# The opening of a two-layer decoder trunk: first input block in two transfers, its weights on another queue, products on half the tokens

## The chip, the cores and the metric

The kernel runs on one core of a Trainium2 chip. The metric is the device time of one execution in microseconds (us). Several executions are timed and their median counts; one more execution is recorded by the hardware profiler, and every row shown here comes from such a record.

## The reference

Two layers of a causal decoder trunk on 512 tokens of width 1024. Only the start matters here: the input is normalized by its root mean square, scaled by a gain per channel, and multiplied with the input weights of layer 0.

```python
def rms_norm(x, g):
    x32 = x.astype(jnp.float32)
    y = x32 * lax.rsqrt(jnp.mean(x32 * x32, axis=-1, keepdims=True) + EPS)
    return y.astype(x.dtype) * g

# layer 0, with x of shape (1, 512, 1024) and w_in_even[0] of shape (1024, 2048)
xn = rms_norm(h, norm_mix[0])
proj = jnp.einsum('bsd,de->bse', xn, w_in_even[0])
z_b = proj[..., 3 * A_WIDTH:]          # columns 1536 to 2047: computed first by the kernel
...
# then: gated convolution and causal pooling, an output projection, a gated ConvFFN;
# layer 1: chunked spatial gating and a second gated ConvFFN; a final rms_norm
```

All of it is float32.

## The kernel before

A product of two float32 matrices is made of three products of 32-bit values rounded for TensorE ("fp32r"): each operand is split into a high part (`hi`, a rounded copy) and a low part (`lo`, the rest), and high x high, high x low and low x high are added up in a PSUM bank. Splitting is work for ScalarE and VectorE.

The first stage computes z, columns 1536 to 2047 of the projection, channel by token: four PSUM banks `z`, one for each 128 columns, each of 512 tokens. The sum runs over eight blocks of 128 input channels. For a block k the kernel

- loads `xt`, the block's 128 channels of all 512 tokens (token-major, four groups of 128 tokens), and `raw_z`, the block's 128 x 512 weights (`load`, L373); blocks 0 and 1 alone, the others in pairs;
- turns the block channel-major by four TensorE transposes (`turn`, L390, transposes at L399);
- splits it, scaled by the gain: high part on ScalarE (L419), low part on VectorE (L432), into `hg`; the unscaled block is copied to `h` (L440);
- splits the weights into `whi_z` and `wlo_z` (L422, L426, L417 for the high part, L414 for the low part);
- issues its twelve products, four banks times three kinds. For blocks 0 and 1 these are written out in `z_first` (L452, products at L459), kind by kind, with the next block's `turn` between the first kind and the second; later blocks go through `group` (L163) and `mm3` (L158).

The normalization's factor is applied to z afterwards, so the sums of squares are gathered beside the products (L209).

The first block differs. Its gain column comes in a small transfer of its own (`first_gain`, L366), since the table of all gains (`pkmix`, L104) has to be transposed on TensorE first (L110). Its turned block lies in two banks of 256 tokens: ScalarE scales the second half while VectorE rounds the weights (L422) and then scales the first half (L424). Its products wait for both halves.

Before any data is there, TensorE multiplies a tile `idle` that VectorE has cleared (L56): eight fillers of 512 columns at the start and three of 256 after the first transposes (`keep_busy`, L58):

```python
WARM = (8, 512)
STAY = (3, 256)
```

The order on each engine is fixed by hand in this stage: whatever passes through `inorder` keeps its place in the program's order on its engine. The transfers of the stage are issued by SP, those of `first_gain` and `pkmix` by ScalarE's queue. Transfers take turns on eight semaphores, so an issue can wait for the transfer eight places earlier.

Of the kernel before, what the change touches and what calls it, by code (L numbers as in the profile page):

```python
# [22 lines left out]
EPS = 1e-6  # L23
WINDOWS = (2, 4, 8, 16)
PAD = 16
WARM = (8, 512)
STAY = (3, 256)
LINE = 64


# [1 line left out]
def tile_trunk(ctx: ExitStack, tc: tile.TileContext, x, norm_mix, norm_ffn, final_norm,  # L32
# [19 lines left out]
    inorder = tc.keep_in_program_order  # L52


    idle = tp.tile([P, 512], BF16, tag="rstd", name="idle")
    nc.vector.memset(idle, 0.0)  # L56

    def keep_busy(bank, n, cols):  # L58

        for i in range(n):  # L60
            inorder(nc.tensor.matmul(bank[:, :cols], idle[:, :P], idle[:, :cols], start=i == 0,
                                     stop=i == n - 1))

    keep_busy(aux_bank("clock"), *WARM)
# [23 lines left out]

    eps = small[:, 1:2]
    nc.gpsimd.memset(eps, EPS)  # L90
    nc.scalar.activation(tp.tile([P, LINE], F32, tag="sd", bufs=1, name="sd_0")[:, :1], eps, AF.Sqrt)
# [4 lines left out]
    def params(layer, rows_, order=lambda ins: ins):  # L96
        return params_fetch(layer, rows_, nc.sync)(order)

    def params_fetch(layer, rows_, queue):
        rows = sum(n for _, _, n in rows_)  # L100
        pk = cp.tile([P, P], F32, tag="pk", bufs=1, name=f"pk{layer}")
        at, views = 0, {}
        for key, ap, n in rows_:
            queue.dma_start(pk[at : at + n, :], ap)  # L104
            views[key] = at
            at += n

        def turned(order=lambda ins: ins):
            ps = aux_bank(f"prm_ps{layer}")
            order(nc.tensor.transpose(ps[:, :rows], pk[:rows, :], ident[:rows, :rows]))  # L110
# [16 lines left out]
        return ap.rearrange("w (r p) -> (w r) p", p=P)  # L127


    def fetch(src, a, b, name):  # L130
        raw = wp.tile([P, a, b], F32, tag="raw", bufs=4, name=f"raw_{name}")
        nc.sync.dma_start(raw, src)
        return raw, a, b, name

    def weights(src, a, b, name):
# [22 lines left out]
    def mm3(ps, lhs, rhs, start, stop):  # L158
        nc.tensor.matmul(ps, lhs[0], rhs[0], start=start, stop=False)  # L159
        nc.tensor.matmul(ps, lhs[0], rhs[1], start=False, stop=False)  # L160
        nc.tensor.matmul(ps, lhs[1], rhs[0], start=False, stop=stop)  # L161

    def group(name, outs, ks, lhs, rhs, tail, on_done, before=None, at_end=None, begun=None):  # L163

        start, banks = begun or (0, {})
        head = max(0, len(ks) - tail)
        order = [(i, j) for i in range(start, head) for j in outs]  # L170
        order += [(i, j) for j in outs for i in range(head, len(ks))]
        at = start - 1
        for i, j in order:
            if i > at and before is not None:
                before(ks[i])
            at = max(at, i)
            if j not in banks:
                banks[j] = mm_bank(f"{name}_{j}")
            mm3(banks[j], lhs(ks[i], j), rhs(ks[i], j), i == 0, i == len(ks) - 1)
# [144 lines left out]

    prm0 = prm1 = None

    def in_fetch(name, w, c0, k, n):
        return fetch(w[k * P : (k + n) * P, c0 : c0 + 512].rearrange("(k p) c -> p k c", p=P),
                     n, 512, f"{name}_{k}")

    def in_parts(chunks, k, raw, after=(None, None)):
        hi, lo = parts(*raw, after=after)
# [28 lines left out]
    def mixer0():  # L361
        nonlocal prm0
        w = w_in_even[0]
        with tc.tile_pool(name="m0", bufs=1) as mp:
            first_gain = tp.tile([P, LINE], F32, tag="ms", bufs=1, name="first_gain")[:, :1]
            nc.scalar.dma_start(first_gain, norm_mix[0][:P].rearrange("(p o) -> p o", o=1))  # L366
            prm_mix = {"turned": params_fetch("mix", [("mix", rows_of(norm_mix[0]), NK)],
                                              nc.scalar)}
            norm = Norm("m0", lambda k: prm_mix["col"]("mix", k))
            zchunks = {}  # L370
            xt = {}

            def load(k, n):  # L373
                t = mp.tile([P, NT, n * P], F32, tag="four", bufs=5, name=f"xt{k}")
                nc.sync.dma_start(
                    t, x[:, k * P : (k + n) * P].rearrange("(t p) d -> p t d", p=P))
# [7 lines left out]
            def put_square(ins):  # L384
                fed[1] = inorder(ins)

            for k, n in ((0, 1), (1, 1), (2, 2), (4, 2)):
                load(k, n)

            def turn(k):  # L390
                order = inorder if k < 3 else lambda ins: ins
                split_at = HALF if k == 0 else S
                banks = [mm_bank(f"xt_ps{k}_{i}") for i in range(S // split_at)]

                def turned_(cs):
                    return banks[cs.start // split_at][:, cs.start % split_at :][:, : cs.stop - cs.start]

                for t in range(NT):
                    order(nc.tensor.transpose(turned_(slice(t * P, (t + 1) * P)), xt[k][:, t, :],  # L399
                                              ident))  # L400
                pieces = [slice(i, i + split_at) for i in range(0, S, split_at)]
                if k == 0:
                    keep_busy(mm_bank("busy"), *STAY)
                if k in raws:
                    raw, a, b, name = raws.pop(k)
                    hi = wp.tile([P, a, b], F32R, tag="whi", bufs=6, name=f"whi_{name}")
                    lo = wp.tile([P, a, b], F32R, tag="wlo", bufs=6, name=f"wlo_{name}")
                    for i in range(a):
                        zchunks[k + i] = hi[:, i, :], lo[:, i, :], raw[:, i, :]
                whi, wlo, wraw = zchunks[k]  # L410
                g = prm_mix["col"]("mix", k) if k else first_gain

                def low_weights():
                    inorder(nc.vector.tensor_tensor(wlo, wraw, whi.bitcast(F32), ALU.subtract))  # L414

                if k > 2:
                    inorder(nc.scalar.activation(whi, wraw, AF.Copy))  # L417
                for cs in pieces[-1:]:
                    inorder(nc.scalar.activation(hg[k][0][:, cs], turned_(cs), AF.Copy, scale=g))  # L419
                if k == 0:  # L420
                    for cs in (slice(0, 256), slice(256, 512)):
                        inorder(nc.vector.tensor_copy(whi[:, cs], wraw[:, cs]))  # L422
                    cs = pieces[0]
                    inorder(nc.vector.tensor_scalar_mul(hg[k][0][:, cs], turned_(cs), g))  # L424
                elif k <= 2:
                    inorder(nc.scalar.activation(whi, wraw, AF.Copy))  # L426
                else:
                    low_weights()
                if k == 0:
                    low_weights()  # L430
                for cs in pieces:
                    fed[0] = inorder(nc.vector.scalar_tensor_tensor(  # L432
                        hg[k][1][:, cs], turned_(cs), g, hg[k][0].bitcast(F32)[:, cs],
                        op0=ALU.mult, op1=ALU.subtract))
                if 0 < k <= 2:
                    low_weights()
                if k == 0:
                    prm_mix["col"] = prm_mix["turned"](inorder)
                for cs in pieces:
                    inorder(nc.vector.tensor_copy(h[k][:, cs], turned_(cs)))  # L440
                if k > 0:
                    norm.square(k - 1, put_square)
                if k == 0:
                    load(6, 2)
                elif k == NK - 1:
                    norm.square(k, put_square)

            def ahead(k):
# [3 lines left out]
            def z_first():  # L452

                banks = {j: mm_bank(f"z_{j}") for j in range(4)}
                turn(0)
                for k in range(2):
                    for n, (l, r) in enumerate(((0, 0), (1, 0), (0, 1))):
                        for j in range(4):
                            inorder(nc.tensor.matmul(  # L459
                                banks[j], zchunks[k][l][:, j * P : (j + 1) * P], hg[k][r],  # L460
                                start=k == n == 0, stop=False))
                        if n == 0:
                            turn(k + 1)
                return banks
# [1138 lines left out]
```

## Time and profile before

| | us |
|---|---|
| median of 3 timed runs | 967.64 |
| the three runs | 967.56, 967.64, 969.01 |
| the profiled execution's own time | 967.45 |
| its span, first to last instruction | 965.7 |
| TensorE busy in the span | 956.8 |
| first real product starts, in the span | 6.07 |

Times inside the profile count from the start of the span. A row of the timeline gives start, length, engine, line and operation, the tile written and the tiles read, the shape and the count, and in brackets the idle time before it with what ended it. PE is TensorE's products, PEld its weight loads, DVE is VectorE, ACT is ScalarE; SPq and ACTq are the queues of SP and ScalarE on which transfers are issued.

### The profile page before, as it was taken

The numbers are of one execution on the slowest core, as the hardware profiler recorded it, in microseconds if no ns is written. First come the engines' busy times: TensorE is split into PE (matmuls) and PEld (weight loads), VectorE is DVE, ScalarE is ACT, GpSimd is POOL, SyncE is SP. The second block draws the span as 40 slices with busy tenths as digits, with TensorE's granted clock in tenths as the row PEclk, the third lists the DMA queues.
The fourth block names the chain that finished last, engine by engine and source line by source line (L and its number), as shares of the span: only waits on it lengthen the run. The fifth ranks groups of instructions, "written<-read, shape, count | busy, mean of one in ns | idle before, by whom it ended". The sixth has DMA issues, their size and how long they took to land.

```text
span 965.7 us, 14233 instructions
## 1 busy us (share of the span) xinstructions
PE 956.8 (99%) x5152; PEld 827.2 (86%) x5152; DVE 847.4 (88%) x1437; ACT 621.6 (64%) x942; POOL 162.5 (17%) x184
## 2 busy tenths in 40 slices
PE   9999999999999999999999999999999999999996
PEld 7888898998888888888888888989888888888885
DVE  6887988989899998998878689889998989889897
ACT  5524667766576565765487847787665666646776
POOL 2142323111011010110311002311111011100123
PEclk9999999999999999999999999999999999999998
DMA  7442345777677577774352323467767777657775
GB/s 253 147 140 87 66 145 118 176 191 191 162 179 177 147 177 193 170 179 133 130 153 88 109 88 88 142 142 176 187 150 190 193 175 174 177 150 196 196 153 142
DMA packets 95538, 150.47 MB, mean 156 GB/s; under 512 B 5252, under 2 KB 61036, under 8 KB 95468
## 3 DMA queue, kind: packets, MB, share of 16 engines
q1 hardware_dynamic: 78140, 98.69, 31.2%
q0 software_dynamic: 15696, 49.03, 28.0%
q10 hardware_dynamic: 1632, 1.84, 0.6%
q8 instruction: 41, 0.67, 0.3%
q14 instruction: 29, 0.24, 0.1%
HBM read 98.42 MB, written 2.10 MB: 104 GB/s over the span
## 4 chain that ended last, share of the span: by engine, by line
PE 99%; DVE 1%; ACT 0%; issue 0%; ACTq 0%
PE dn L159 3%; PE d L159 3%; PE dn L160 3%; PE d L160 3%; PE d L161 3%; PE dn L161 3%; PE vu_a L1145 2%; PE gu L159 2%; PE gu L161 2%; PE gu L160 2%; PE u_2a L696 1%; PE g_2a L696 1%; PE u_4a L696 1%; PE u_20a L686 1%; PE u_16a L686 1%; PE u_18a L686 1%
## 5 line engine op out<-in xcount | busy, mean ns | idle before, releaser
L146 POOL DMA_DIRECT2D wlo_g<-raw_g x20 | 17.2, 860 | 312.3 <-DVE kept L923 142.6
L732 DVE SCALAR_TENSOR_TENSOR c<-rows,prm,c 128x512 f32<-128x512 f32 x88 | 65.5, 747 | 1.7 <-ACT c L730 1.4
L159 PE MATMUL d<-a_hi,whi_d 128*128 128x512 f32 x144 | 56.1, 390 | 0.0
L159 PE MATMUL dn<-whi_dn,a_hi 128*128 128x512 f32 x144 | 56.1, 390 | 0.0
L160 PE MATMUL d<-a_lo,whi_d 128*128 128x512 f32 x144 | 56.1, 390 | 0.0
L160 PE MATMUL dn<-wlo_dn,a_hi 128*128 128x512 f32 x144 | 56.1, 390 | 0.0
L161 PE MATMUL d<-a_hi,wlo_d 128*128 128x512 f32 x144 | 56.1, 389 | 0.0
L161 PE MATMUL dn<-whi_dn,a_lo 128*128 128x512 f32 x144 | 56.1, 389 | 0.0
L847 ACT ACTIVATE whi_a<-raw_g 128x512 fp32r<-128x512 f32 x20 | 12.6, 631 | 61.0 <-PE g_10e L686 8.5
L730 ACT ACTIVATE c<-rows,prm 128x512 f32<-128x512 f32 x44 | 31.4, 716 | 14.9 <-DVE rows L947 14.9
L1350 DVE SCALAR_TENSOR_TENSOR y<-dn,small,y 128x512 f32<-128x512 f32 x40 | 28.0, 749 | 7.9 <-PE dn L161 7.8
L740 ACT ACTIVATE s<-c,prm 128x512 f32<-128x512 f32 x44 | 31.4, 716 | 3.3 <-DVE c L732 3.3
L155 DVE TENSOR_TENSOR wlo_dn<-raw_dn,whi_dn 128x1024 fp32r<-128x1024 f32 x18 | 22.0, 1223 | 11.5 <-ACT whi_dn L154 11.5
L204 ACT ACTIVATE hg<-h,prm 128x512 fp32r<-128x512 f32 x24 | 17.2, 719 | 22.9 <-DVE h L317 17.0
L161 PEld LDWEIGHTS dn<-whi_dn,a_lo 128*128 128x128 f32 x144 | 27.0, 188 | 5.6
L161 PEld LDWEIGHTS d<-a_hi,wlo_d 128*128 128x128 f32 x144 | 27.1, 188 | 5.6
L159 PEld LDWEIGHTS dn<-whi_dn,a_hi 128*128 128x128 f32 x144 | 27.1, 188 | 5.6
L160 PEld LDWEIGHTS d<-a_lo,whi_d 128*128 128x128 f32 x144 | 27.1, 188 | 5.6
L160 PEld LDWEIGHTS dn<-wlo_dn,a_hi 128*128 128x128 f32 x144 | 27.1, 188 | 5.5
L159 PEld LDWEIGHTS d<-a_hi,whi_d 128*128 128x128 f32 x144 | 27.1, 188 | 5.5
L268 ACT ACTIVATE a_hi<-s 128x512 fp32r<-128x512 f32 x40 | 24.7, 625 | 10.7 <-PE d L161 9.4
L144 ACT ACTIVATE wlo_g<-raw_g 128x1024 fp32r<-128x1024 f32 x20 | 20.9, 1048 | 16.3 <-PE g_2e L696 7.7
(1274 smaller groups left out, 3380.9 us busy)
## 6 DMA issues: line engine op xcount, KB each, us to landing
raw_g<-in_w_ffn_gate_dram SPq DMA_DIRECT2D x40, 512.0 KB, 3.6
raw_u<-in_w_ffn_up_dram SPq DMA_DIRECT2D x40, 512.0 KB, 4.3
raw_dn<-in_w_ffn_down_dram SPq DMA_DIRECT2D x22, 512.0 KB, 4.5
wlo_g<-raw_g POOLq DMA_DIRECT2D x20, 512.0 KB, 4.6
wlo_u<-raw_u POOLq DMA_DIRECT2D x20, 512.0 KB, 5.8
raw_d<-in_w_ffn_down_dram SPq DMA_DIRECT2D x18, 512.0 KB, 4.1
wlo_s12g<-s12g POOLq DMA_DIRECT2D x18, 512.0 KB, 5.3
wlo_s34g<-s34g POOLq DMA_DIRECT2D x18, 512.0 KB, 5.0
```

Of the source, the lines that this page charges most:

```text
L144: first = nc.scalar.activation(lo, raw, AF.Copy, scale=-1.0)
L155: behind(nc.vector.tensor_tensor(lo, raw, hi.bitcast(F32), ALU.subtract), after[0])
L159: nc.tensor.matmul(ps, lhs[0], rhs[0], start=start, stop=False)
L160: nc.tensor.matmul(ps, lhs[0], rhs[1], start=False, stop=False)
L161: nc.tensor.matmul(ps, lhs[1], rhs[0], start=False, stop=stop)
L268: nc.scalar.activation(hi, src, AF.Copy, scale=scale)
L686: last_matmul[0] = nc.tensor.matmul(ps if low else banks[at], left(kp)[low], right(kp)[0] if low else both(kp), start=first, stop=kp == NP ...
L696: nc.tensor.matmul(ps, l, r, start=first, stop=end, skip_group_check=True)
L730: nc.scalar.activation(c, t[:, 0:S], AF.Copy, scale=prm("cf", ft))
L732: self.last_conv = nc.vector.scalar_tensor_tensor(c, t[:, i : S + i], prm("cf", i * NF + ft), c, op0=ALU.mult, op1=ALU.add)
L740: self.last_silu = nc.scalar.activation(s, c, AF.Silu, bias=self.prm("bf", ft))
L1350: return nc.vector.scalar_tensor_tensor(dst, ps, ffn.cols[:, t : t + 1], dst, op0=ALU.mult, op1=ALU.add)
```

## The change

The change concerns the first block of the z stage and what comes before it.

- The fillers read a constant (1.0 in bfloat16, broadcast) that is set up with the program, and the tile `idle` with its clearing goes. There are six of 512 columns, not eight, and two of 256, not three.
- Block 0 is loaded in two transfers of 256 tokens each, both from SP. The block's weights are issued on ScalarE's queue, between the gain column and the gain table; on SP their place is taken by the second half.
- `turn_first` takes the place of `turn(0)`. TensorE's order is: two transposes of the first half, two fillers, two transposes of the second half, four products of 128x256 on the first half, four on the second, the transpose of the gain table, then the second block's transposes. Before, it was four transposes, three fillers, the gain table, four products of 128x512, the second block's transposes.
- VectorE scales the first half first and then rounds the right half of the weights; ScalarE rounds the left half of the weights and then scales the second half of the block. Before, VectorE rounded both halves of the weights first, and ScalarE none.
- The small square root that loads ScalarE's table is issued after the three transfers on that queue.

The diff, cut to its core:

```diff
-WARM = (8, 512)
-STAY = (3, 256)
+WARM = (6, 512)
+STAY = (2, 256)
...
-    idle = tp.tile([P, 512], BF16, tag="rstd", name="idle")
-    nc.vector.memset(idle, 0.0)
-
     def keep_busy(bank, n, cols):
 
         for i in range(n):
-            inorder(nc.tensor.matmul(bank[:, :cols], idle[:, :P], idle[:, :cols], start=i == 0,
+            inorder(nc.tensor.matmul(bank[:, :cols], nc.const_aps.tensor(1.0, [P, P], BF16),
+                                     nc.const_aps.tensor(1.0, [P, cols], BF16), start=i == 0,
                                      stop=i == n - 1))
...
             def load(k, n):
                 t = mp.tile([P, NT, n * P], F32, tag="four", bufs=5, name=f"xt{k}")
-                nc.sync.dma_start(
-                    t, x[:, k * P : (k + n) * P].rearrange("(t p) d -> p t d", p=P))
+                rows = x[:, k * P : (k + n) * P].rearrange("(t p) d -> p t d", p=P)
                 for i in range(n):
                     xt[k + i] = t[:, :, i * P : (i + 1) * P]
-                raws[k] = in_fetch("z", w, 1536, k, n)
+                if k == 0:
+                    inorder(nc.sync.dma_start(t[:, :2], rows[:, :2]))
+                    raws[k] = in_fetch("z", w, 1536, k, n, nc.scalar, inorder)
+                    inorder(nc.sync.dma_start(t[:, 2:], rows[:, 2:]))
+                    return
+                inorder(nc.sync.dma_start(t, rows))
+                raws[k] = in_fetch("z", w, 1536, k, n, nc.sync, inorder)
...
+            def turn_first(banks):
+                chunk(0)
+                whi, wlo, wraw = zchunks[0]
+                halves = [slice(0, HALF), slice(HALF, S)]
...
+                def high_products(i):
+                    for j in range(4):
+                        inorder(nc.tensor.matmul(
+                            banks[j][:, halves[i]], whi[:, j * P : (j + 1) * P],
+                            hg[0][0][:, halves[i]], start=i == 0, stop=False,
+                            skip_group_check=True))
+
+                transposed(0)
+                inorder(nc.vector.tensor_scalar_mul(hg[0][0][:, halves[0]], turned_[0], first_gain))
+                keep_busy(mm_bank("busy"), *STAY)
+                inorder(nc.scalar.activation(whi[:, halves[0]], wraw[:, halves[0]], AF.Copy))
+                inorder(nc.vector.tensor_copy(whi[:, halves[1]], wraw[:, halves[1]]))
+                transposed(1)
+                high_products(0)
+                inorder(nc.scalar.activation(hg[0][0][:, halves[1]], turned_[1], AF.Copy,
+                                             scale=first_gain))
+                inorder(nc.vector.tensor_tensor(wlo, wraw, whi.bitcast(F32), ALU.subtract))
+                high_products(1)
+                for i in range(2):
+                    low_part(0, turned_[i], first_gain, halves[i])
+                prm_mix["col"] = prm_mix["turned"](inorder)
+                for i in range(2):
+                    inorder(nc.vector.tensor_copy(h[0][:, halves[i]], turned_[i]))
+                load(6, 2)
...
-                turn(0)
+                turn_first(banks)
                 for k in range(2):
                     for n, (l, r) in enumerate(((0, 0), (1, 0), (0, 1))):
-                        for j in range(4):
-                            inorder(nc.tensor.matmul(
-                                banks[j], zchunks[k][l][:, j * P : (j + 1) * P], hg[k][r],
-                                start=k == n == 0, stop=False))
+                        if n or k:
+                            for j in range(4):
+                                inorder(nc.tensor.matmul(
+                                    banks[j], zchunks[k][l][:, j * P : (j + 1) * P], hg[k][r],
+                                    start=False, stop=False, skip_group_check=True))
```

More of the change, by code (lines that the diff above doesn't have):

```diff
@@ L97, in params, with params_fetch @@
         return params_fetch(layer, rows_, nc.sync)(order)
-    def params_fetch(layer, rows_, queue):
+    def params_fetch(layer, rows_, queue, first=lambda ins: ins):
         rows = sum(n for _, _, n in rows_)
@@ L103, in params_fetch @@
         for key, ap, n in rows_:
-            queue.dma_start(pk[at : at + n, :], ap)
+            first(queue.dma_start(pk[at : at + n, :], ap))
             views[key] = at
@@ L127, in conv_rows, with fetch @@
         return ap.rearrange("w (r p) -> (w r) p", p=P)
-    def fetch(src, a, b, name):
+    def fetch(src, a, b, name, queue=nc.sync, order=lambda ins: ins):
         raw = wp.tile([P, a, b], F32, tag="raw", bufs=4, name=f"raw_{name}")
-        nc.sync.dma_start(raw, src)
+        order(queue.dma_start(raw, src))
         return raw, a, b, name
@@ L385, in put_square, with chunk @@
                 fed[1] = inorder(ins)
-            for k, n in ((0, 1), (1, 1), (2, 2), (4, 2)):
-                load(k, n)
+            load(0, 1)
+            prm_mix["turned"] = params_fetch("mix", [("mix", rows_of(norm_mix[0]), NK)], nc.scalar,
+                                             inorder)
+            inorder(nc.scalar.activation(work("sd", 1, "0"), eps, AF.Sqrt))
+            for k, n in ((1, 1), (2, 2), (4, 2)):
+                load(k, n)
+            def chunk(k):
+                raw, a, b, name = raws.pop(k)
+                hi = wp.tile([P, a, b], F32R, tag="whi", bufs=6, name=f"whi_{name}")
+                lo = wp.tile([P, a, b], F32R, tag="wlo", bufs=6, name=f"wlo_{name}")
+                for i in range(a):
+                    zchunks[k + i] = hi[:, i, :], lo[:, i, :], raw[:, i, :]
@@ new lines, in low_part, with transposed @@
+            def low_part(k, ps, g, cs=slice(0, S)):
+                return inorder(nc.vector.scalar_tensor_tensor(
+                    hg[k][1][:, cs], ps, g, hg[k][0].bitcast(F32)[:, cs],
+                    op0=ALU.mult, op1=ALU.subtract))
+            def turn_first(banks):
+                chunk(0)
+                whi, wlo, wraw = zchunks[0]
+                halves = [slice(0, HALF), slice(HALF, S)]
+                turned_ = []
+                for c in halves:
+                    ps = mm_bank(f"xt_ps0_{c.start}")[:, :HALF]
+                    turned_.append(ps)
+                def transposed(i):
+                    for t in range(2):
+                        inorder(nc.tensor.transpose(turned_[i][:, t * P : (t + 1) * P],
+                                                    xt[0][:, 2 * i + t, :], ident))
+                def high_products(i):
[21 more added lines that the diff above has]
+                load(6, 2)
@@ L390, in turn @@
             def turn(k):
                 order = inorder if k < 3 else lambda ins: ins
[L392 to L396, printed above, removed]
+                ps = mm_bank(f"xt_ps{k}")
                 for t in range(NT):
-                    order(nc.tensor.transpose(turned_(slice(t * P, (t + 1) * P)), xt[k][:, t, :],
-                                              ident))
@@ L401, in turn @@
-                pieces = [slice(i, i + split_at) for i in range(0, S, split_at)]
-                if k == 0:
-                    keep_busy(mm_bank("busy"), *STAY)
-                if k in raws:
[L405 to L409, printed above, removed]
+                    order(nc.tensor.transpose(ps[:, t * P : (t + 1) * P], xt[k][:, t, :], ident))
@@ L410, in turn @@
+                if k in raws:
+                    chunk(k)
                 whi, wlo, wraw = zchunks[k]
-                g = prm_mix["col"]("mix", k) if k else first_gain
+                g = prm_mix["col"]("mix", k)
                 def low_weights():
@@ L417, in turn @@
                     inorder(nc.scalar.activation(whi, wraw, AF.Copy))
[L418 to L425, printed above, removed]
+                inorder(nc.scalar.activation(hg[k][0], ps, AF.Copy, scale=g))
+                if k <= 2:
                     inorder(nc.scalar.activation(whi, wraw, AF.Copy))
@@ L428, in turn @@
                     low_weights()
-                if k == 0:
+                fed[0] = low_part(k, ps, g)
+                if k <= 2:
                     low_weights()
[L431 to L445, printed above, removed]
+                inorder(nc.vector.tensor_copy(h[k], ps))
+                norm.square(k - 1, put_square)
+                if k == NK - 1:
                     norm.square(k, put_square)
```

18 lines of the change are left out of this document (8 added, 10 removed).

## The prediction

> **What bounds the kernel now.** I read the page first, then the chain of work that ended last, TensorE's waits, and the timeline of the first 13 us.
>
> ```profile
> span 965.7 us, 14233 instructions
> ...
> PE 956.8 (99%) x5152; PEld 827.2 (86%) x5152; DVE 847.4 (88%) x1437; ACT 621.6 (64%) x942; POOL 162.5 (17%) x184
> ...
> PE 99%; DVE 1%; ACT 0%; issue 0%; ACTq 0%
> ```
>
> TensorE is busy for 956.8 of 965.7 us and carries 99% of the chain. So a change counts only where TensorE is not yet on real work, or where it is made to wait. The chain in order of time shows where that is:
>
> ```profile
> 0.93 0.28 DVE idle L56
> ...
> 1.26 3.60 PE clock L61 x8
> 4.85 0.67 PE xt_ps L399 x4
> ...
> 5.54 0.48 ACT hg L419
> ...
> 6.07 1.19 PE z L459 x4
> ...
> 7.70 2.76 PE z L459 x12
> ```
>
> The columns are start, length, and what the end hangs on. VectorE clears the tile "idle", eight fillers run on it, four transposes of the first input block follow, ScalarE splits half of the result, and only at 6.07 does the first real product start. After that it is product upon product. The waits of TensorE's weight loads over the whole span say the same:
>
> ```profile
> PEld L61 <- issue: 1.7, 6, 0.3
> PEld L61 <- DVE idle L56: 1.3, 1, 1.3
> PEld xt_ps L399 <- issue: 0.5, 2, 0.3
> PEld wst L1257 <- DVE wsT L1262: 0.3, 1, 0.3
> ```
>
> All but 0.3 us of the large ones lie in the opening. What the change is worth is therefore the shift of one instruction: the first transpose of the second block, from which on both kernels issue the same TensorE instructions in the same order (I compared the built streams of all five engines; the later ones differ only in which earlier DMA some issues wait for).
>
> **The change part by part.** The rows of the opening, with the DMA issues:
>
> ```profile
> 0.80 0.45 ACTq L366 DMA_DIRECT2D first_gain<-in_norm_mix_dram  x1
> 0.81 0.43 SPq L375 DMA_DIRECT2D xt<-in_x_dram  x1
> 1.29 1.28 ACT L91 ACT_TABLE_LOAD   x1 [1.29 <-PEq L1589]
> 1.30 0.49 SPq L132 DMA_DIRECT2D raw_z<-in_w_in_even_dram  x1
> 1.35 0.60 ACTq L104 DMA_DIRECT2D pkmix<-in_norm_mix_dram  x1
> ...
> 4.22 0.23 PEld L399 LDWEIGHTS xt_ps<-ident,xt 128*128 128x128 f32 x1 [0.27 <-issue]
> ...
> 4.65 0.86 PE L399 MATMUL xt_ps<-ident,xt 128*128 128x128 f32 x4
> ...
> 4.81 0.49 DVE L422 CAST whi_z<-raw_z 128x256 fp32r<-128x256 f32 x2 [3.61 <-DMA raw_z<-in_w_in_even_dram]
> ...
> 5.32 0.48 DVE L424 TENSOR_SCALAR hg<-xt_ps,first_gain 128x256 fp32r<-128x256 f32 x1
> 5.34 0.49 PE L61 MATMUL busy<-idle 128*128 128x256 bf16 x3
> 5.54 0.47 ACT L419 ACTIVATE hg<-xt_ps,first_gain 128x256 fp32r<-128x256 f32 x1 [2.76 <-PE xt_ps L399]
> 5.72 0.68 DVE L414 TENSOR_TENSOR wlo_z<-raw_z,whi_z 128x512 fp32r<-128x512 f32 x1
> ...
> 5.76 0.22 PE L110 MATMUL prm_psmix<-ident,pkmix 8*128 8x8 f32 x1
> ...
> 6.32 0.87 DVE L432 SCALAR_TENSOR_TENSOR hg<-xt_ps,first_gain,hg 128x256 fp32r<-128x256 f32 x2
> ...
> 7.10 0.60 PE L399 MATMUL xt_ps<-ident,xt 128*128 128x128 f32 x4
> ...
> 8.32 0.62 ACT L426 ACTIVATE whi_z<-raw_z 128x512 fp32r<-128x512 f32 x1
> ```
>
> Prices per instruction come from the groups by line (count, then busy us and mean ns of one), and from the first and last of ten half-width products in a row:
>
> ```profile
> L61 PE MATMUL clock<-idle 128*128 128x512 bf16 x8 | 3.6, 631 | 1.3 <-DVE idle L56 1.3
> L61 PE MATMUL busy<-idle 128*128 128x256 bf16 x3 | 0.5, 272 | 0.0
> L579 ACT ACTIVATE t<-ybr 128x256 fp32r<-128x256 f32 x8 | 3.1, 405 | 0.3 <-DVE ybr L603 0.3
> ...
> 122.75 0.28 PE L696 MATMUL oe_10a<-ya_hi,whi_oe 128*128 128x256 f32 x1
> ...
> 123.82 0.28 PE L696 MATMUL oe_10a<-ya_hi,whi_oe 128*128 128x256 f32 x1
> ```
>
> Fillers: eight in 3.60 us, the last 0.63 long, so (3.60 - 0.63) / 7 = 0.424 us from one to the next. Without the clear, the wait on VectorE goes: fillers can start when VectorE started, near 0.96, not 1.26. Six end at 0.96 + 6 x 0.424 = 3.50; in the kernel before the eighth ended at 4.65. The block's weight load at 4.22 shows that the data was there by then, so the last filler was in the way.
>
> Two transfers for the first block: each is 131 KB. How far the bytes are, by the stretches (last column GB/s, which over 1 us is KB):
>
> ```profile
> 1.00:2.00 1.00, 0.74 (x2) 0.28 (x3) 0.20 (x1) 0.71 (x1) 0.96 (x27) 1.00 0.04 11
> 2.00:3.00 1.00, 1.00 (x4) 0.36 (x3) 0.00 (x0) 0.77 (x2) 0.20 (x1) 1.00 0.71 146
> 3.00:4.00 1.00, 1.00 (x4) 0.39 (x3) 0.00 (x0) 0.00 (x0) 0.00 (x0) 1.00 1.04 337
> 4.00:5.00 1.00, 1.00 (x4) 0.58 (x3) 0.19 (x1) 0.00 (x0) 0.00 (x0) 1.00 1.00 293
> ```
>
> Block and weights are 524 KB. 11 + 146 + 337 = 494 KB have moved at 4.00, so they were through at 4.1; VectorE took the weights at 4.81, 0.7 later, which I take as the lag from bytes to landing. The first half, 131 KB, is through at 2.82 and lands at 3.5, just as the six fillers end. Second half and weights now come over two queues: together through at 4.1, landed at 4.8; the one that is served first lands at 4.0 (half, 262 KB) or 4.4 (weights, 393 KB). I take 4.6 for both, between the ends, and keep 4.0 to 4.8. The row on which this rests is one stream on one queue; a second queue is in no row here except for the small gain and parameter loads.
>
> The Trainium skill, "DMA: Bandwidth & Descriptors", section "Issuing engines are not separate DMA queues", says that transfers started from different engines run on the same 16 DMA engines and interleave, and that a second issuer saves only issue time. By that rule the new queue brings no bytes sooner, both pieces land at 4.8, and the sum below comes out at 0.5 us, not 0.7.
>
> The sum. First-half transposes: 3.55 to 3.98. (Two at 0.21: four take 0.44 in the later chain, 0.11 each, and the fillers show half that rate at this point: 0.424 for 512 columns, against (0.49 - 0.27) / 2 = 0.11 for 256 at 5.34.) VectorE scales them from about 4.25 for 0.48, to 4.73, then copies half of the weights, half of 0.49, to 5.0. Two fillers of 256 columns fill TensorE to 4.4. Second-half transposes run 4.6 to 5.03, readable at 5.25. ScalarE splits the other weight half at 4.65 for 0.41, to 5.06, then the second half of the block from 5.28 for 0.47, to 5.75. First four half-width products: 5.1 to 5.7, at (123.82 - 122.75) / 9 = 0.12 each when the clock is up, 0.21 before. Second four: 5.8 to 6.3. The parameter transpose, which moves from ahead of the products to behind them, comes on the path now: 0.22 alone, of which most is pipeline that the next transposes overlap, so 0.1. So the second block's transposes start at 6.4 and no longer at 7.10: 0.7 us gained. Eight half products cost 8 x 0.12 = 0.96 where four wide ones took 7.10 - 6.07 = 1.03, so halving them is free at the full clock.
>
> Is anything late at 6.4? The second block's own transfer:
>
> ```profile
> L375 SPq DMA_DIRECT2D xt<-in_x_dram x1: 427/427/427, 1.8 to 1.8; - x1
> ...
> DMA to landing us min/median/max: 4.3/4.3/4.3
> ```
>
> Issued at 1.84, landed at 6.14, with the same bytes ahead of it in both kernels: in time by 0.26, and this is the ceiling of the gain: 7.10 - 6.2 = 0.9. VectorE's low part of the weights (0.68 from 5.06) and of the block (0.87) are done at 6.6, ahead of the products that read them at 6.85 and 7.8. ScalarE's first use of the second block's weights at 8.32 would move to about 7.6; when those land is not shown, only that it is by 8.32, and TensorE wants them at 6.4 + 0.44 + 8 x 0.23 = 8.7 (2.76 / 12 = 0.23 for a wide product). If they land at 8.3 the split ends at 8.9 and 0.2 is lost. On ScalarE's queue the weights' issue (0.5) goes ahead of parameters (0.60) and table load (1.28), which then end near 3.9, before 4.6: hidden by the wait for the weights, and 1:1 on the path if that wait were over 0.7 shorter. On SP every issue behind the first block stays in its place, as one half replaces the weights; later issues wait for an older DMA one place sooner (the third weights for the gain vector), behind a queue with megabytes to move. VectorE loses the clear (0.28) and half a copy, off the path.
>
> So the shift is 0.7 us, at least 0 and at most 0.9. The profiled run took 967.45 us with a span of 965.7, 1.75 lying outside; it would become 966.75. The three timed runs have a median of 967.64, 0.19 above it: the forecast is 967.64 - 0.7 = 966.9.
>
> **The rivals.** *The clock opens late* (slower). The kernel before gets the full clock between 4.65 and 5.34, after 3.39 us of fillers and the transposes. The changed one has 2.54 us of fillers, 0.43 more after the transposes, and waits around them. If the clock then comes one such stretch later, 5.2 + 3.4 = 8.6, everything between goes at half rate: products 5.1 to 5.95 and 5.95 to 6.8, transposes 6.9 to 7.75, then two wide products at 0.42 by 8.6. The kernel before stands at 8.6 with (8.6 - 7.7) / 0.23 = 3.9 of them: 1.9 x 0.23 = 0.4 us behind, 968.0. It decides once the clock opens after about 7.8. Two stretches later, 12.0, cost another 3.4 / 2 = 1.7: 969.7. For it: fewer fillers, and 969.01 among the three times, 1.4 above the others. Against it: the fillers start 0.3 sooner, and TensorE idles nowhere for long. The Trainium skill, "TensorE: Matmul & The Clock Gate", Part 1, has the half clock released after about 3.4 us of sustained activity, in a window that runs free of the kernel, and Part 4 says that transposes do not count as activity in the same way. By that rule a stretch with 2.5 us of fillers need not open it and this rival is the likely case; the trace agrees on the 3.4 us, but shows one phase of the window only.
>
> *The weights come late over ScalarE's queue.* They stand behind the gain vector, 128 pieces of 4 bytes. Landed at 5.8 they eat the whole gain, and from there each us costs one: 6.8 gives 968.6. Against it: the gain is used at 5.32 at the latest.
>
> *Nothing moves*: halves and weights take turns so that both land at 5.3, or the second block slips to 6.9: 967.6.
>
> **How the numbers follow.** Forecast 0.50, with a range of its own of 966.6 to 967.3. Clock late by one stretch 0.16, by two 0.07. Late weights 0.08, half of it over 2 us. Nothing moves 0.14. Faster by what no row shows 0.05. 0.2% is 1.9 us, about what a measurement of this kernel can tell from no change. Faster than 965.7 would need the products at 4.1, where the data is not there: 0.05. Slower than 969.6: 0.07 + 0.04 = 0.11. Within: 0.84. The range leaves out those two and runs from 966.2 (the ceiling of 0.9 and a spread of 0.5) to 968.9 (late clock, late weights of 1 us).
>
> **What would show it.** Right: fillers from 0.96, ending near 3.5; half-width products from 5.1, 0.12 apart by 5.8; the second block's first transpose near 6.4; a span of 965.0. Wrong: products 0.21 or 0.42 apart after 6, VectorE's or ScalarE's first weight split after 5.0, or TensorE waiting for the second block.

## The result, and the profile after

The change makes the kernel slower: 970.59 us (median of ten runs, 969.62 to 971.84) against 967.71 (967.24 to 969.01). The ratio is 1.0028, with a 95% interval of 1.002 to 1.0036. The forecast was 966.9, with a range up to 968.9.

The profiled execution took 971.11 us. From the page after, the span, TensorE's busy time and the shares of the chain:

```profile
span 969.3 us, 14238 instructions
...
PE 958.8 (99%) x5153; PEld 828.5 (85%) x5153; DVE 846.4 (87%) x1435; ACT 621.8 (64%) x943; POOL 162.4 (17%) x184
...
PE 98%; DMA 1%; DVE 1%; ACT 0%; issue 0%; SPq 0%; ACTq 0%
```

A transfer has entered the chain. Its order of time (start, length, what the end hangs on) shows which:

```profile
0.81 0.44 SPq L375
...
1.30 5.26 DMA xt<-in_x_dram
...
6.61 0.69 PE xt_ps L418 x2
7.30 1.79 PE z L423 x8
9.09 0.20 PE prm_psmix L107
9.29 1.04 PE xt_ps L450 x4
10.34 3.63 PE z L486 x12
13.96 0.44 PE xt_ps L450 x4
...
16.68 0.23 PE z L156
```

Two rows of the same view before, not shown yet, mark the same places:

```profile
10.47 0.44 PE xt_ps L399 x4
...
13.20 0.24 PE z L159
```

The third block's first product comes at 16.68 instead of 13.20: 3.48 of the 3.6 us between the two spans are lost by then. They have two sources. The second half of the first block lands at 1.30 + 5.26 = 6.56, so real products start late. And they run slowly: the second block's transposes take 1.04 instead of 0.44, the next twelve products 3.63 instead of 2.76. The timeline after shows both:

```profile
0.84 2.72 PE L58 MATMUL clock<-const-bfloat16-1.0 128*128 128x512 bf16 x6 [0.84 <-PEq L1616]
...
1.28 0.45 ACTq L129 DMA_DIRECT2D raw_z<-in_w_in_even_dram  x1
1.30 0.48 SPq L377 DMA_DIRECT2D xt<-in_x_dram  x1
...
3.60 0.66 PE L418 MATMUL xt_ps<-ident,xt 128*128 128x128 f32 x2
...
4.05 0.63 PE L58 MATMUL busy<-const-bfloat16-1.0 128*128 128x256 bf16 x2
...
5.79 0.42 ACT L431 ACTIVATE whi_z<-raw_z 128x256 fp32r<-128x256 f32 x1 [1.91 <-DMA raw_z<-in_w_in_even_dram]
...
6.61 0.69 PE L418 MATMUL xt_ps<-ident,xt 128*128 128x128 f32 x2 [1.92 <-DMA xt<-in_x_dram]
...
6.95 2.14 PE L423 MATMUL z<-hg,whi_z 128*128 128x256 f32 x8
...
9.99 2.06 PE L486 MATMUL z<-hg,wlo_z 128*128 128x512 f32 x4
...
11.84 2.12 PE L486 MATMUL z<-hg,whi_z 128*128 128x512 f32 x8
```

Weights at 5.79 where VectorE had them at 4.81 before; TensorE idle for 1.92 us ahead of the second half; four wide products still in 2.06 us at 9.99, and eight in 2.12 only at 11.84. So TensorE ran at half its rate until near 12, where before it was at full rate by 5.34. I call this change of rate the opening of the clock: wide products stand 0.42 apart before it and 0.23 after it.

### The profile page after: what moved, and what is told of

The parts are those of the page before. It is cut to its first block, busy times and chain, and to the rows that moved or that the text cites. A ratio compares the mean times of both kernels' runs of the same rounds, so it can differ in the third digit from the quotient of the medians.

```text
span 969.3 us, 14238 instructions
## 1 busy us (share of the span) xinstructions
PE 958.8 (99%) x5153; PEld 828.5 (85%) x5153; DVE 846.4 (87%) x1435; ACT 621.8 (64%) x943; POOL 162.4 (17%) x184
## 4 chain that ended last, share of the span: by engine, by line
PE 98%; DMA 1%; DVE 1%; ACT 0%; issue 0%; SPq 0%; ACTq 0%
PE d L156 3%; PE dn L156 3%; PE dn L157 3%; PE d L157 3%; PE d L158 3%; PE dn L158 3%; PE vu_a L1172 2%; PE gu L156 2%; PE gu L158 2%; PE gu L157 2%; PE u_2a L723 1%; PE g_2a L723 1%; PE u_4a L723 1%; PE u_14a L713 1%; PE u_8a L713 1%; PE u_16a L713 1%
```

## The experiments

Each was compared with the kernel before on the same chip (its median in brackets, over 31 to 33 runs; 11 runs of each experiment, nine of e10). The times of single runs hold 1.7 to 2.0 us outside the span, now and then 2.3 to 3.5, so the spans of the timed runs stand beside them. For the change itself they are 967.9 to 969.6, and 965.5 to 966.9 for the kernel before (three of its 97 runs lie above, at 967.3, 968.2 and 968.4). One run of e11, of 2294 us, stands far apart and is left out of its spans.

| run | transfers of block 0 | fillers 512, 256 wide | us (before) | ratio, 95% | spans |
|---|---|---|---|---|---|
| e1 | halves, weights, all SP | 6, 2 | 969.68 (967.85) | 1.0007 to 1.0025 | 966.4 to 969.3 |
| e2 | as changed | 6, 12 | 968.56 (967.85) | 0.9998 to 1.0016 | 966.4 to 967.6 |
| e3 | as before | 6, 2 constant | 968.79 (967.85) | 1.0002 to 1.002 | 965.6 to 967.9 |
| e4 | weights on ScalarE's queue | 8, 3 cleared | 969.20 (967.85) | 1.0009 to 1.0026 | 966.7 to 971.1 |
| e5 | as before | 8, 3 constant | 968.33 (968.03) | 0.9994 to 1.0011 | 965.5 to 967.0 |
| e6 | one block, weights, SP | 8, 4 | 967.70 (968.03) | 0.9985 to 1.0003 | 965.3 to 966.2 |
| e7 | half, weights, half, SP | 6, 6 | 968.30 (968.03) | 0.9997 to 1.0014 | 966.2 to 968.4 |
| e8 | halves, weights, all SP | 6, 10 | 969.15 (968.03) | 1.0002 to 1.0019 | 966.6 to 967.3 |
| e9 | as changed | 9, 2 | 968.62 (967.97) | 1.0000 to 1.0018 | 966.5 to 967.2 |
| e10 | as changed | 6, 2 | 969.96 (967.97) | 1.0016 to 1.0035 | 966.9 to 969.9 |
| e11 | one block, weights, SP | 8, 8 | 968.74 (967.97) | 1.0000 to 1.0019 | 965.8 to 966.9 |
| e12 | as before | 2, 2 cleared | 969.77 (967.97) | 1.0007 to 1.0025 | 966.2 to 969.6 |

### Is it the transfers or the fillers? (e1 to e4)

The theory (A) at this point: the weights' own queue holds back the second half, and the late clock follows from the wait. The rival (B): six and two fillers are too few whatever the transfers do.

**e1**, on the changed kernel:

```diff
                     inorder(nc.sync.dma_start(t[:, :2], rows[:, :2]))
-                    raws[k] = in_fetch("z", w, 1536, k, n, nc.scalar, inorder)
                     inorder(nc.sync.dma_start(t[:, 2:], rows[:, 2:]))
+                    raws[k] = in_fetch("z", w, 1536, k, n, nc.sync, inorder)
```

> The changed kernel, but with the first block's weights issued by SP again, behind both halves. Theory A (the weights on ScalarE's queue push the second half back, and the half clock follows from the wait): the second half lands near 4.1 us instead of 6.56, the weights near 4.8, the second block's transposes start near 6.5, the clock opens within the opening, time near 967.2 (0.3 to 0.7 under the kernel before). Theory B (six and two fillers are too few, whatever the transfers do): the second half is early, but products still stand 0.21 or 0.42 us apart until 8 us or later, time 968 to 969.5. Theory C (two transfers are slow in themselves): the second half still lands after 5.5, time near 970.5.

Timeline of TensorE, and one row of the chain:

```profile
4.26 0.38 PE L418 MATMUL xt_ps<-ident,xt 128*128 128x128 f32 x2
6.20 1.22 PE L423 MATMUL z<-hg,whi_z 128*128 128x256 f32 x8 [1.56 <-ACT whi_z L431]
7.35 0.22 PE L107 MATMUL prm_psmix<-ident,pkmix 8*128 8x8 f32 x1
...
1.83 3.88 DMA raw_z<-in_w_in_even_dram
```

The second half is there when TensorE is ready for it, at 4.26, so theory C, which had it land after 5.5 here too, falls. But the weights, now last on SP, land at 5.71, and the runs scatter in two heaps: six spans from 966.4 to 966.9, five from 968.0 to 969.3. The profiled run is of the first heap and has eight half products in 1.22 us, the full clock. A alone does not explain the second.

**e2**, on the changed kernel:

```diff
-STAY = (2, 256)
+STAY = (12, 256)
```

> The changed kernel with twelve 256-column fillers between the two pairs of transposes instead of two: ten more at 0.21 us fill TensorE to about 6.1 us at the half clock. The transfers stay as they are. Theory A and B alike: the clock opens near 5 us as in the kernel before, the second half still lands near 6.5, and what is left is the late landing alone: second block's transposes near 8.2 instead of 9.22, time near 968.8 (1.1 over the kernel before). If the clock were not the larger part, the time would stay near 970.5.

Timeline, then two rows of the chain:

```profile
4.09 1.87 PE L58 MATMUL busy<-const-bfloat16-1.0 128*128 128x256 bf16 x12
...
1.30 4.78 DMA xt<-in_x_dram
...
8.02 0.59 PE xt_ps L450 x4
```

The second half is late as in the change (6.08 here, 6.56 there, 6.05 when the change ran again as e10), yet 2.2 of the change's 2.9 us are gone, and so is the scatter. The second block's transposes come at 8.02, near the 8.2 expected. What is left, 968.56 - 967.85 = 0.7 us, I put down to the landing, on which the chain hangs; its interval holds 1.

**e3**, on the kernel before: the tile `idle` goes, and

```diff
-WARM = (8, 512)
-STAY = (3, 256)
+WARM = (6, 512)
+STAY = (2, 256)
...
-            inorder(nc.tensor.matmul(bank[:, :cols], idle[:, :P], idle[:, :cols], start=i == 0,
+            inorder(nc.tensor.matmul(bank[:, :cols], nc.const_aps.tensor(1.0, [P, P], BF16),
+                                     nc.const_aps.tensor(1.0, [P, cols], BF16), start=i == 0,
```

> The kernel before with only the filler part of the change: six of 512 and two of 256 columns on the constant, no cleared tile, everything else as before. Theory B: the clock opens one stretch of 3.4 us later in some or all runs, time 968 to 970. Theory A: fillers end at 3.4, the first block's transposes start at its landing near 4.1 instead of 4.65, TensorE waits about 0.7 us at most, the clock opens as before, time 967.2 to 967.7.

```profile
4.16 0.79 PE L397 MATMUL xt_ps<-ident,xt 128*128 128x128 f32 x4 [0.60 <-DMA xt<-in_x_dram]
...
7.14 0.63 PE L397 MATMUL xt_ps<-ident,xt 128*128 128x128 f32 x4
```

The transposes start at the landing, 4.16 and not 4.65, as A expected. At the second block nothing is left of it (7.14 against 7.10). Three spans lie at 965.6 to 965.9, as in the kernel before, eight at 966.8 to 967.9: with nothing but the fillers changed the median rises by 0.9 us. B holds, though the profiled run is one of the three early ones: that the late heap is the clock is argued here and not shown.

**e4**, on the kernel before: the load's weights, with the gain table and the table load behind them on that queue as in the change,

```diff
-                raws[k] = in_fetch("z", w, 1536, k, n)
+                raws[k] = in_fetch("z", w, 1536, k, n, nc.scalar if k == 0 else nc.sync, inorder)
```

> The kernel before with only the queue part of the change: the first block's weights issued on ScalarE's queue between the gain column and the gain table, the block itself in one transfer, eight and three fillers on the cleared tile. Theory A: the weights' larger packets go ahead of the block's, which lands at 6 us or later instead of before 4.22; the eight fillers keep TensorE at work to 4.65, so the clock opens by 8 at the latest; time 968.5 to 970. Theory B: the transfer order matters little, time 967.4 to 968.2.

A row of the chain and two of the timeline:

```profile
1.29 5.29 DMA raw_z<-in_w_in_even_dram
...
0.81 0.98 SPq L373 DMA_DIRECT2D xt<-in_x_dram  x2
...
4.64 1.06 PE L401 MATMUL xt_ps<-ident,xt 128*128 128x128 f32 x4
```

The cost is in the expected range, the mechanism is not mine: the block is on time (transposes at 4.64), and the weights themselves land at 6.58, where SP's queue brings them by 4.81. On ScalarE's queue the same 256 KB, issued at the same moment, come 1.8 us later. The queue is not all that differs: SP issues the second block (the second xt of its row) where it issued the weights before, so that block's bytes now run beside the weights. Which of the two costs the time was not tried apart.

### What the clock asks for (e5, e8, e9, e10, e12)

**e5** is e3 with `WARM = (8, 512)` and `STAY = (3, 256)`.

> The kernel before with eight and three fillers as it was, but reading the constant, with no cleared tile: against e3 only the number of fillers differs, against the kernel before only what they read and that they start at 0.84 instead of 1.26. If the number of fillers and the hole behind them set when the clock opens (theory B as it stands now), the runs lie as close together as those of the kernel before, median 967.4 to 968.0. If the constant itself opens the clock later than the cleared tile does, they scatter up to 970 as in e3, median above 968.5.

The median of the times missed both figures, 968.33, between them; the spans, 965.5 to 967.0, are those of the kernel before, and e3's heap up to 967.9 is gone. So the constant is not at fault, and the number of fillers is what is left.

**e8** is e1 with `STAY = (10, 256)`.

> e1 (both halves, then the weights, on SP) with ten 256-column fillers between the pairs of transposes instead of two, so that the hole of 1.56 us before the first product closes at the half clock. If the scatter of e1 (968.1 to 971.3) is the clock, it goes: all runs within 968.0 to 968.8, median near 968.3, the weights landing at 5.7 being what is left over the kernel before. If it is something in the transfers, the scatter stays.

e1's second heap is gone (966.6 to 967.3). The median, 969.15, is over 0.8 above what I expected, and the interval is 0.2 to 1.8 us over the kernel before, though the spans' median of 966.9 is only 0.7 above its 966.2; the other 0.4 lies outside the span. I expected 0.3 for the weights' landing, and it is about 0.7.

**e9** and **e10** ran together; e10 is the change unaltered, e9 differs in one number:

```diff
-WARM = (6, 512)
+WARM = (9, 512)
```

> The changed kernel with nine 512-column fillers instead of six, two of 256 as it has: TensorE is at work without a break from 0.84 to about 4.7 us, and then waits for the second half until about 6.3. Theory B1 (3.4 us of work from whatever start open the clock): it opens near 4.3 in every run, the wait of 1.6 us does not close it, runs between 968.0 and 969.2, median 968.6 as in e2. Theory B2 (the 3.4 us stretches run on by themselves and one must be filled from end to end): 3.9 us fill one only when it happens to start early enough, so many runs stay late and scatter from 968.5 to 971.5, median 969.5 to 970.5.

> The changed kernel unaltered, for a second profile and ten more times beside the others. Theories B1 and B2: the clock opens at 8 us or later here too, products 0.42 us apart for 512 columns until then, the second half lands at 6.0 us or later, median 970.1 to 971.1.

TensorE's timeline in e9:

```profile
0.84 3.74 PE L58 MATMUL clock<-const-bfloat16-1.0 128*128 128x512 bf16 x9 [0.84 <-PEq L1616]
4.42 0.38 PE L418 MATMUL xt_ps<-ident,xt 128*128 128x128 f32 x2
...
5.54 0.44 PE L418 MATMUL xt_ps<-ident,xt 128*128 128x128 f32 x2 [0.52 <-DMA xt<-in_x_dram]
6.64 1.22 PE L423 MATMUL z<-hg,whi_z 128*128 128x256 f32 x8 [0.66 <-ACT whi_z L431]
...
8.36 1.17 PE L486 MATMUL z<-hg,wlo_z 128*128 128x512 f32 x4
```

and in e10, with a row of its chain:

```profile
6.66 2.07 PE L423 MATMUL z<-hg,whi_z 128*128 128x256 f32 x8
...
9.64 2.06 PE L486 MATMUL z<-hg,wlo_z 128*128 128x512 f32 x4
...
1.30 4.75 DMA xt<-in_x_dram
```

Real products start at the same place, 6.64 and 6.66, behind transfers issued alike. Eight half products take 1.22 us in e9 and 2.07 in e10, four wide ones 1.17 and 2.06. Three more fillers, worth 1.3 us of TensorE's idle time, bring the median from 969.96 to 968.62, and the spans of all eleven runs into 966.5 to 967.2, where e10's nine spread over 3 us. (e10's own median lies just under the 970.1 to 971.1 expected, and two times of e9 lie above 969.2, with spans of 966.5 and 966.6.) The outcome is B1's: with 3.7 us of work in one piece the clock opens early (in this run by 4.42, the two transposes 0.38 - 0.27 = 0.11 apart), and the two waits behind it, 0.52 and 0.66, do not close it. B2 as I put it, with a stretch to be filled from end to end, is refuted by e1's profile: 2.72 us of fillers were enough there. The change, too, has work from 0.84 to 4.68, as long as that, but with the two transposes of 0.66 in the middle of it.

**e12** is the kernel before with `WARM = (2, 512)` and `STAY = (2, 256)`.

> The kernel before with two 512-column fillers instead of eight and two of 256 instead of three: the transfers, the order of the work and the tile that the fillers read are untouched, only TensorE has no work from 2.1 us to the landing of the first block near 4.1. If the late clock alone can cost what the change cost, the runs rise and scatter, median 969.5 to 971; products 0.42 apart until 8 us or later in the profile. If the clock is not what costs, the time stays at 967.4 to 967.9, since the first block's transposes start 0.5 sooner.

```profile
4.13 1.08 PE L399 MATMUL xt_ps<-ident,xt 128*128 128x128 f32 x4 [1.84 <-DMA xt<-in_x_dram]
...
5.87 2.04 PE L459 MATMUL z<-hg,whi_z 128*128 128x512 f32 x4
...
8.42 1.39 PE L459 MATMUL z<-hg,wlo_z 128*128 128x512 f32 x4
9.65 2.00 PE L459 MATMUL z<-hg,whi_z 128*128 128x512 f32 x8
```

The first product is even 0.2 earlier than before (5.87), the transfers are untouched, and the kernel loses 1.8 us: four wide products take 2.04 at first, the next four 1.39, as the clock opens among them, and then eight take 2.00. The late clock alone costs nearly two thirds of what the change cost.

The traces also record the granted clock, which the readings above infer from the products. The record begins with the opening, and the time before it is counted as full: so the clock column of the rows by stretches (third from the end) reads 1.00 even where TensorE ran at half rate, and shows nothing there. The full clock begins at 5.17 us in the kernel before, 12.12 in the change, 12.17 in e10, 8.90 in e12, 6.49 in e5, 4.51 in e3, 4.18 in e9 and 3.84 in e1. In all fourteen profiles it lasts 952.32, 955.73 or 959.14 us, that is 279, 280 or 281 steps of 3.413. So opening and closing lie on a grid of such steps, and the kernel starts at no fixed place in one: counted back from the opening, the first line of the grid is at 0.4 in e1, at 1.9 in the change, at 3.1 in e5.

How much work opened it can be estimated from TensorE's rows, transposes left out. The step that ended in the opening held at least 2.37 us of work in each of the fourteen profiles (2.37 in e7, 2.72 in e1, 3.34 in e9), and no earlier step held more than 2.32 (from 1.88 to 5.29 in the change). So the estimate is some 2.35 of 3.41 us; whether transposes count is open, since with them the two sides part as well, at 2.78 and 2.77. By this, e1 opened early and the change late in their profiles, with the same six fillers, because the grid lay differently. It does not explain all: with every place of the grid as likely as another, the same count would have the change open early in about six runs of ten, and of its 19 timed runs at most one (span 966.9) did. Whether its wait of 1.92 us closes the clock again is shown by no profile.

### Order of the transfers, and a better version (e6, e7, e11)

**e7** is the change with the weights on SP between the halves (`nc.scalar` becomes `nc.sync`) and `STAY = (6, 256)`.

> The changed kernel with the weights on SP between the two halves, and six 256-column fillers between the pairs of transposes. If a queue of its own is what puts the weights ahead, the second half, which now stands behind them on one queue, lands near 4.8 and the weights near 4.4; products from 5.1, time 967.2 to 968. If the order alone matters, the second half lands near 6 as in the changed kernel, time 968.5 to 969.5.

A row of VectorE's timeline and one of the chain:

```profile
4.83 0.29 DVE L432 CAST whi_z<-raw_z 128x256 fp32r<-128x256 f32 x1
...
1.81 3.90 DMA xt<-in_x_dram
```

The time fits neither range well: 968.30, spans mostly 966.2 to 966.7. The weights are there by 4.83, the second half, last in line, lands at 5.71, between the two expectations. If two transfers on one queue cost anything, it is 0.2 to 0.3 us here; the interval holds 1.

**e6** is the change with the block in one transfer:

```diff
-                    inorder(nc.sync.dma_start(t[:, :2], rows[:, :2]))
-                    raws[k] = in_fetch("z", w, 1536, k, n, nc.scalar, inorder)
-                    inorder(nc.sync.dma_start(t[:, 2:], rows[:, 2:]))
+                    inorder(nc.sync.dma_start(t, rows))
+                    raws[k] = in_fetch("z", w, 1536, k, n, nc.sync, inorder)
```

and `WARM = (8, 512)`, `STAY = (4, 256)`.

> A version to beat both: the changed kernel's split of the work (products on 256 tokens, ScalarE and VectorE sharing the weights), but the first block in one transfer and its weights behind it on SP, as before, and eight fillers of 512 and four of 256 columns on the constant. Block at 4.1 and weights at 4.8 as in the kernel before; products from 5.3, the second block's transposes at 6.2 to 7.0 as that block lands; clock open by 5.5. Time 967.0 to 967.7. If the second block lands at 7.0, as in e3, no gain: 967.7.

It has the lowest median of all, 967.70 against 968.03, the upper end of what was expected, but its interval holds 1. In its profiled run the weights come late although they are issued as in the kernel before:

```profile
1.30 4.45 DMA raw_z<-in_w_in_even_dram
```

**e11** is e6 with `STAY = (8, 256)`.

> e6 with eight 256-column fillers between the pairs of transposes instead of four, so that TensorE waits less than 0.6 us before the first product. If the short wait left in e6 still costs some runs their clock, the highest of the runs falls below 968.0 and the median to 967.4 to 967.6; if not, median 967.6 to 968.0 as in e6.

A miss both ways: 968.74, with three spans at 965.8 and five at 966.7 to 966.9. More fillers did not help. The cause was not tried; the weights' landing, which differs from one run to the next, may be it. No version clearly beats the kernel before.

## Why the prediction was wrong

Its likeliest case was wrong in two steps, and both went the same way.

**The landing.** The step "I take 4.6 for both, between the ends" failed; in the profiled run the second half landed at 6.56 and the weights by 5.79. The ends of 4.0 and 4.8 came from bytes at the rate of one stream plus a lag of 0.7. The rows after show the rate itself lower in the same stretches (the last three columns are the clock, the share of the DMA engines and GB/s):

```profile
3.00:4.00 1.00, 0.96 (x4) 0.42 (x3) 0.00 (x0) 0.86 (x2) 0.00 (x0) 1.00 1.00 202
4.00:5.00 1.00, 0.69 (x4) 0.15 (x1) 0.48 (x1) 0.00 (x0) 0.00 (x0) 1.00 1.07 202
```

202 and 202 GB/s, where 337 and 293 stood, with the DMA engines as busy as before (1.00 and 1.07).

The packets by queue show more. ScalarE's queue went first for a while: the packets that started on it from 3.0 to 3.5 held 127 KB, those on SP's queue, with the second half, 8. And each wait ended only behind a tail: of the weights' 128 packets of 2 KB 110 had started by 4.0 in the change, but the last six only after 5.0; in e4 118 by 5.0, the last ten from 5.5 to 6.2. A sum of bytes at a mean rate does not hold such a tail. The sum took the second queue as free; e4, with the difference named there, had the weights land 1.8 us later in the profiled run.

The rule I weighed, of the Trainium skill, "DMA: Bandwidth & Descriptors", section "Issuing engines are not separate DMA queues", was right as far as it goes: neither the weights nor the second half came sooner. That they come later it does not say. Why the rate falls and the last packets lag was not settled. With the clock out of the way what is left of the cost is 0.7 us (e2) or 0.65 (e9: 968.62 - 967.97). The rival of late weights had this too cheap: "Landed at 5.8 they eat the whole gain" does not fit the 5.3 of "Nothing moves", and in e1, with weights at 5.71 and the clock open, the second block's transposes start at 7.51, already 0.4 behind the 7.10 of before.

**The clock.** The forecast rested on "the fillers start 0.3 sooner, and TensorE idles nowhere for long". They did start sooner (0.84), but TensorE then stood still for 1.92 us, and its first fillers came to 2.72 us of work where the kernel before had 3.60. The rival "the clock opens late" is what happened, by two stretches in the profiled run (12.12, against the 12.0 of the rival), and I gave that case 0.07, and 0.23 together with one stretch. Its price for two stretches, 969.7, was near: 970.59 less 0.7 for the landing is 969.9. What was missing is that it comes on top of the late landing and in part from it. The prediction held the two as alternatives, and left the case of two stretches out of its range, which so ended at 968.9. Of the change's 2.9 us, e2 puts 0.7 on the landing and the rest on the clock; e10 and e9, in one group, 0.65 and 1.34 of e10's 1.99. That the rest is the clock is what the records of the opening show for the profiled runs; for the others it is inferred from their spans.

The Trainium skill, "TensorE: Matmul & The Clock Gate", Part 1, spoke for this rival: about 3.4 us of sustained work release the clock, in a window that runs on by itself. The traces agree on the window: the records above lie on steps of 3.413 us that do not start with the kernel, and the same kernel can so open early in one run and late in another, which fits e1, e3 and e12, whose spans spread over 2 to 3.4 us. That the window has to be filled they do not bear out, with 2.72 us of fillers enough in e1. That transposes do not count in the same way, as its Part 4 has it, fits the profiles, but so does counting them.

**What held.** Six fillers ended in time for the first half, whose transposes ran at 3.60 (3.55 in the sum). At the full clock halving the products cost little: 1.15 us in e1 from the first of eight (6.20) to the gain table (7.35), against 1.03 for four wide ones. The shift of the opening is the shift of the end: 3.48 of 3.6. The second block's landing never came into question, since TensorE was later still.

## What to carry to other kernels

Fillers ahead of the first data do two jobs: they pass the time, and they buy the clock. Count them against the second job (here 3.7 us in one piece held in all eleven runs, 2.7 held in some runs only, since it depends on where a run starts), and keep them when the data comes sooner or later. More is safer: by the estimate above even 3.7 us can miss with an unlucky start, about one in six. Before a transfer is cut in two or moved to another queue, ask what lands last, and sum late landing and late clock together, because one brings the other.

## What the runs showed of the hardware

The same transfer of 256 KB, issued at 1.3 us, landed by 4.81 on SP's queue before, at 5.75 on SP's queue in e6, and at 6.58 on ScalarE's queue in e4. The fillers on the constant start at 0.84, 0.4 before those on the cleared tile, and e5's spans are still those of the kernel before: by itself the earlier start shows no gain. The full clock begins and ends on a grid of 3.413 us that does not start with the kernel; a step of it with 2.37 us of work, transposes left out, was enough to open it (e7), one with 2.32 was not (the change).
